# 512-column blocks for v, k, q and the output product, and the gate's modulation on TensorE

## The chip, the cores and the metric

One core of a Trainium2 chip runs one layer of a hybrid network as one program. The metric is the time of one execution on the device in microseconds (us), lower is better. Before the change three runs took 1288.12 to 1289.84 us, with a median of 1289.26 us.

## The reference, cut to what matters

All arithmetic is f32. There are 384 tokens (128 of a prompt with modulation vector `c_ctx`, 256 of a sample with `c`), `D_MODEL` is 2048, and the products below are the ones that the change touches.

```python
mod = jax.nn.silu(cond) @ w_ada + b_ada              # (2048) @ (2048, 6144)
shift, scale, gate = jnp.split(mod[:, None, :], 3, axis=-1)
proj = (_rms(x, norm_w) * (1 + scale) + shift) @ w_in
u, z_s, q, k, v, z_a, g_s, g_a = jnp.split(proj, cuts, axis=-1)   # q, k, v: 1024 columns each
q = _rms(q.reshape(n, L, N_HEADS, HEAD_DIM), q_norm_w)             # 16 heads of 64
k = _rms(k.reshape(n, L, N_HEADS, HEAD_DIM), k_norm_w)
...                                                    # state space branch, attention branch
merged = sigmoid(g_s) * p_s + sigmoid(g_a) * p_a
return x + gate * (merged @ w_o)                        # w_o: (2048, 2048)
```

## The kernel before

Every large product is cut into blocks of 256 output columns, and the list `blocks` gives the order in which TensorE goes through them: the rest of the gate columns (`gs`), v, `ga`, `za`, k and q in turn, then `glu`, `ps` (the state space output), `pa` (the attention output) and `wo` (the output product). A block reads its weights in units of 512 KB; a unit has two halves, and one half is one step of the main loop at the end of `hybrid`.

An f32 product is made from three fp32r products. `Stream.prep` (lines 59 to 66) splits each half of weights into a high part `hi` (a copy on ScalarE, line 64) and a low part `lo` (a subtraction, line 65), and the activations were split earlier into `hh` and `hl`. TensorE then adds high by high, high by low and low by high in PSUM. `mode_b` (lines 174 to 188) holds the weights still and moves 384 tokens past them. `mode_a` (lines 190 to 203) holds 128 tokens still and moves the weights; it serves v, k, q and wo. In `mode_a` a half is two slices of 128 rows by 256 columns, for three token tiles: 18 matmuls of 256 columns. The three token tiles share two PSUM banks of the pool `psm`, which has three; two tiles lie side by side in the first.

The low part is made on VectorE, except where `low_on_pool` is set: in the first stage and from `pa` on it is made on GpSimd.

Other work is written as generators and is put between the steps by `Background.step`: after each step every generator emits what is due, and `finish` drains one at once. The attention starts a head every two steps, once the k, q and v blocks that hold it are there. `split_ys` reads the state space result back and splits it for `glu`; it is started in the middle of the last q block, and `enter("glu")` calls `finish` on it. `keep` normalises one k or q block and turns it.

The gate's part of the modulation (2048 columns of `w_ada`, for both vectors) runs beside `pa` and `wo`. In `gate_step` (line 1269) a `w_ada` tile `gw` of 512 KB is loaded every second step, and each step does two VectorE operations `acc = gw * ct + acc` of 128x512, one for each vector; after 16 steps `gate_rows` splits `acc`, sums its 128 rows with a matmul against ones, and copies the result to `gt`. `evac` of a wo block multiplies the PSUM result by `gt`, adds x and stores it.

All loads and stores named here are issued by SyncE, in program order, in one line.

Of the kernel before, what the change touches and what calls it, by code (L numbers as in the profile page):

```python
# [6 lines left out]
F32 = mybir.dt.float32  # L7
# [27 lines left out]
class Stream:  # L35
# [11 lines left out]
    def load(self, i):  # L47
# [4 lines left out]
        elif kind == "k2":  # L52
            t = t.rearrange("p (k h) c -> p k (h c)", k=2)
            self.nc.sync.dma_start(t, dram(w, k0 * ncol + c0, [[ncol, 128], [128 * ncol, 2], [1, 512]]))
        else:
            self.nc.sync.dma_start(t.rearrange("p k c -> p (k c)"), dram(w, k0 * ncol + c0, [[ncol, 128], [1, 1024]]))
        self.loaded.append(t)

    def prep(self, j):
        i, b = divmod(j, 2)  # L60
        t = self.loaded[i][:, 2 * b:2 * b + 2, :] if self.units[i][4] != "k2" else self.loaded[i][:, :, 256 * b:256 * b + 256]
# [59 lines left out]
def hybrid(ctx, tc, a):  # L121
# [35 lines left out]
    mhalf = const.tile([128, 16], F32, name="mhalf")  # L157
# [32 lines left out]
    def mode_a(i, hb, ps, act, k0, first, last):  # L190

        wh, wl = st.split[2 * i + hb]
        xh, xl = act
        for r in range(3):
            tk = slice(128 * r, 128 * r + 128)
            o = ps[r // 2][:, 256 * (r % 2):256 * (r % 2) + 256]
            for kk in range(2):
                q, j = divmod(k0 + 2 * hb + kk, 4)
                z = last and hb == 1 and kk == 1
                PE.matmul(o, xh[q][:, j, tk], wh[:, kk, :], start=first and hb == 0 and kk == 0 and r != 1, stop=False,  # L200
                          skip_group_check=True)
                PE.matmul(o, xh[q][:, j, tk], wl[:, kk, :], start=False, stop=False, skip_group_check=True)  # L202
                PE.matmul(o, xl[q][:, j, tk], wh[:, kk, :], start=False, stop=z and r != 0, skip_group_check=True)  # L203
# [427 lines left out]

    for j in range(4, 8):
        block("gs", w_in, NIN, 6144 + 256 * j, 4)
    for j in range(4):
        block("v", w_in, NIN, 4096 + 256 * j, 4)
# [4 lines left out]
    for j in range(4):  # L640
        for kind, c0 in (("k", 3072), ("q", 2048)):
            block(kind, w_in, NIN, c0 + 256 * j, 4)
# [6 lines left out]
    for j in range(8):  # L649
        block("wo", a["w_o"], 2048, 256 * j, 4)  # L650
# [243 lines left out]
    def heads_norm(kvt, kr, c0, dst):  # L894

        def gen():
            sq = kvt.tile([128, 3, 256], F32, name="sq", bufs=1)
            r = kvt.tile([128, 12], F32, name="rn")
            r2 = kvt.tile([128, 12], F32, name="rm")
# [8 lines left out]
            tt(k3, k3, r2.unsqueeze(2).to_broadcast([128, 12, 64]), OP.mult)  # L908
            yield -1
            for j in range(2):  # L910
# [4 lines left out]
                dst(2 * c0 + j, p[:, :TOK].rearrange("p (r t) -> p r t", r=3))  # L915
# [4 lines left out]
    def attention(at, kS, kP, qT, vN, aT, ready, done):  # L920
# [118 lines left out]
        while len(start) < NH or tick - start[NH - 1] <= 15:  # L1039
            h = len(start)  # L1040
            if h < NH and (h == 0 or tick - start[h - 1] >= 2) and {("k", h // 4), ("q", h // 4), ("c", h // 4),
                                                                    h // 4} <= ready:
# [37 lines left out]
    def keep(kr, j, kind):  # L1080
        yield from heads_norm(kvt, kr, j, put_k if kind == "k" else put_q)
        M["vd"].add((kind, j))
        if kind == "k":
            kp = kr[:, 1].rearrange("p (h d) -> p h d", d=64)
            tt(kp, kp, kw.unsqueeze(1).to_broadcast([128, kp.shape[1], 64]), OP.mult)
            SP.dma_start(dram(a["out_k"], 256 * j, [[1024, 128], [1, 256]]), kr[:, 1])
# [11 lines left out]
    def evac(kind, c0, ps):  # L1098
        if kind in ("k", "q"):
            j = c0 % 1024 // 256  # L1100
# [3 lines left out]
            g_qk.append(bg.add(keep(kr, j, kind)))  # L1104
            return
        if kind == "v":
            j = c0 % 1024 // 256
            cs = slice(256 * j, 256 * j + 256)
            for r in range(3):
                S.activation(M["v"][r][:, cs], ps[r // 2][:, 256 * (r % 2):256 * (r % 2) + 256], AF.Copy)  # L1110
            SP.dma_start(dram(a["out_v"], 256 * j, [[1024, 128], [1, 256]]), M["v"][1][:, cs])
            M["vd"].add(j)
            return
        if kind == "wo":
            cs = slice(c0, c0 + 256)
            yt = M["gp"].tile([128, 3, 256], F32, name="yt", bufs=2)
            gt = M["gt"]
            for r, (n, t0) in enumerate((("out_s", 0), ("out_p", 0), ("out_s", 128))):
                tt(yt[:, r], ps[r // 2][:, 256 * (r % 2):256 * (r % 2) + 256], gt[:, r % 2, cs], OP.mult)
                tt(yt[:, r], yt[:, r], M["x"][:, r], OP.add)  # L1120
                SP.dma_start(dram(a[n], t0 * D + c0, [[D, 128], [1, 256]]), yt[:, r])
            return
        for c in range(2):
# [25 lines left out]
            elif kind == "pa":  # L1149
# [3 lines left out]
                tt(o, o, t, OP.add, eng=GP)  # L1153

    def enter(kind):
# [38 lines left out]
        elif kind == "pa":  # L1194
# [6 lines left out]
            one = gp.tile([128, 128], F32, name="one")  # L1201
            V.memset(one, 1.0)
            M["ones"] = gp.tile([128, 128], F32R, name="ones")
            S.activation(M["ones"], one, AF.Copy)
            M["bg"] = gp.tile([128, D], F32, name="bg")
            GP.memset(M["bg"], 0.0)
            SP.dma_start(M["bg"][0:1, :], dram(a["b_ada"], 4096, [[D, 1], [1, D]]))
# [61 lines left out]
    def gate_step(t):  # L1269

        gp = M["gp"]
        if t % 2 == 0 and t < 64:
            w = gaw[t // 2] = gp.tile([128, 2, 512], F32, name="gw", bufs=6)
            n, u = divmod(t // 2, 8)
            SP.dma_start(w, dram(a["w_ada"], 256 * u * 6144 + 4096 + 512 * n, [[6144, 128], [128 * 6144, 2], [1, 512]]))
        n, kt = divmod(t - 6, 16)
        if 0 <= n < 4:
            if kt == 0:
                gaw["acc"] = gp.tile([128, 2, 512], F32, name="acc", bufs=2)
            w = gaw[(t - 6) // 2][:, kt % 2]  # L1280
            for m in range(2):
                o = gaw["acc"][:, m]
                stt(o, w, ct[:, kt, m:m + 1], o if kt else M["bg"][:, 512 * n:512 * n + 512], OP.mult, OP.add)
            if kt == 15:
# [89 lines left out]
```

## Time and profile before

| what | value |
|---|---|
| median of 3 runs | 1289.26 us (1288.12 to 1289.84) |
| the profiled execution | 1288.84 us, of which 1287.1 us is the span from first to last instruction |
| TensorE busy | 1200.3 us (93%) |
| VectorE busy | 871.0 us (68%) |
| ScalarE, GpSimd busy | 574.7 us (45%), 326.2 us (25%) |
| mean granted TensorE clock | 0.981 of full speed |

The profile is of one execution. Busy times are sums over the whole span, and stages differ, so a share of the span says little about one stage. The granted clock of 1.00 is 2.4 GHz and 0.50 is 1.2 GHz; a value between them is a mean over a stretch that had both. Matmuls overlap each other, so what one costs is read from the distance between the starts of neighbours, not from its own duration.

### The profile page before, as it was taken

The numbers are of one execution on the slowest core, as the hardware profiler recorded it, in microseconds if no ns is written. First come the engines' busy times: TensorE is split into PE (matmuls) and PEld (weight loads), VectorE is DVE, ScalarE is ACT, GpSimd is POOL, SyncE is SP. The second block draws the span as 40 slices with busy tenths as digits, with TensorE's granted clock in tenths as the row PEclk, the third lists the DMA queues.
The fourth block names the chain that finished last, engine by engine and source line by source line (L and its number), as shares of the span: only waits on it lengthen the run. The fifth ranks groups of instructions, "written<-read, shape, count | busy, mean of one in ns | idle before, by whom it ended". The sixth has DMA issues, their size and how long they took to land.

```text
span 1287.1 us, 22729 instructions
## 1 busy us (share of the span) xinstructions
PE 1200.3 (93%) x8591; PEld 1109.6 (86%) x8591; DVE 871.0 (68%) x1931; ACT 574.7 (45%) x1060; POOL 326.2 (25%) x240
## 2 busy tenths in 40 slices
PE   3999999998999999999999999998999988778998
PEld 3787788897899988989997998987889987778898
DVE  3588765576479943649993446466786479999941
ACT  4432223335853378673349545455554233322231
POOL 2444445541000000000000001000100077766554
PEclk9999999999999999999999999999999999889999
DMA  9975566569264485337443555648673466656642
GB/s 266 349 268 196 199 217 232 162 147 262 68 158 157 140 146 150 95 90 174 151 153 106 155 121 123 103 111 198 172 180 130 156 205 216 221 163 230 228 145 92
DMA packets 256221, 219.97 MB, mean 171 GB/s; under 512 B 81319, under 2 KB 235551, under 8 KB 255727
## 3 DMA queue, kind: packets, MB, share of 16 engines
q1 hardware_dynamic: 255760, 218.33, 58.7%
q8 instruction: 68, 1.11, 0.4%
q0 software_dynamic: 352, 0.20, 0.2%
q14 instruction: 41, 0.34, 0.1%
HBM read 200.30 MB, written 16.87 MB: 169 GB/s over the span
## 4 chain that ended last, share of the span: by engine, by line
PE 68%; DVE 14%; DMA 6%; ACT 5%; issue 4%; SPq 2%; POOL 0%; DVEq 0%; ACTq 0%; POOLq 0%
PE m L186 8%; PE m L188 8%; PE m L187 8%; DVE acc L149 8%; PE m L200 7%; PE m L202 7%; PE m L203 6%; PE m L808 5%; PE m L809 5%; PE m L810 4%; PE bk L688 3%; PE bk L967 2%; DMA sg<-yss 2%; PE bk L443 1%; ACT H L454 1%
## 5 line engine op out<-in xcount | busy, mean ns | idle before, releaser
L64 ACT ACTIVATE hi<-raw 128x512 fp32r<-128x512 f32 x464 | 286.5, 628 | 381.9 <-PE m L203 122.0
L65 POOL TENSOR_TENSOR lo<-raw,hi 128x512 fp32r<-128x512 f32 x191 | 274.0, 1447 | 331.4 <-ACT hi L64 206.0
L65 DVE TENSOR_TENSOR lo<-raw,hi 128x512 fp32r<-128x512 f32 x273 | 186.6, 687 | 180.7 <-ACT hi L64 171.7
L186 PE MATMUL m<-hh,hi 128*128 128x384 f32 x832 | 289.5, 348 | 15.5 <-DVE tgl L149 12.9
L200 PE MATMUL m<-hi,hh 128*128 128x256 f32 x960 | 278.0, 290 | 16.2 <-DVE yt L141 14.3
L188 PE MATMUL m<-hh,lo 128*128 128x384 f32 x832 | 281.7, 339 | 1.0 <-POOL lo L65 0.9
L187 PE MATMUL m<-hl,hi 128*128 128x384 f32 x832 | 281.2, 338 | 0.0
L203 PE MATMUL m<-hi,hl 128*128 128x256 f32 x960 | 273.9, 285 | 1.0 <-DVE hl L149 1.0
L202 PE MATMUL m<-lo,hh 128*128 128x256 f32 x960 | 274.0, 285 | 0.1
L200 PEld LDWEIGHTS m<-hi,hh 128*128 128x128 f32 x960 | 186.3, 194 | 21.8 <-DVE yt L141 15.1
L203 PEld LDWEIGHTS m<-hi,hl 128*128 128x128 f32 x960 | 186.4, 194 | 1.2 <-DVE hl L149 1.2
L202 PEld LDWEIGHTS m<-lo,hh 128*128 128x128 f32 x960 | 186.5, 194 | 0.6 <-DVE lo L65 0.3
L186 PEld LDWEIGHTS m<-hh,hi 128*128 128x128 f32 x832 | 158.1, 190 | 27.6 <-DVE tgl L149 14.8
L188 PEld LDWEIGHTS m<-hh,lo 128*128 128x128 f32 x832 | 158.3, 190 | 2.2 <-POOL lo L65 1.8
L187 PEld LDWEIGHTS m<-hl,hi 128*128 128x128 f32 x832 | 158.5, 191 | 0.1
L808 PE MATMUL m<-hh,hi 128*128 128x384 f32 x384 | 135.1, 352 | 16.3 <-DVE hh L726 7.4
L149 DVE SCALAR_TENSOR_TENSOR acc<-gw,ct,acc 128x512 f32<-128x512 f32 x120 | 144.4, 1265 | 0.0
L809 PE MATMUL m<-hl,hi 128*128 128x384 f32 x384 | 131.2, 342 | 0.8 <-DVE hl L141 0.5
L810 PE MATMUL m<-hh,lo 128*128 128x384 f32 x384 | 130.7, 340 | 0.5 <-POOL lo L65 0.5
L141 POOL TENSOR_TENSOR rm<-rn,mhalf 128x12 f32<-128x12 f32 x8 | 19.1, 2386 | 380.8 <-PE m L203 229.9
L808 PEld LDWEIGHTS m<-hh,hi 128*128 128x128 f32 x384 | 73.1, 190 | 31.7 <-DVE hh L726 8.7
L809 PEld LDWEIGHTS m<-hl,hi 128*128 128x128 f32 x384 | 73.5, 191 | 2.2 <-DVE hl L141 2.2
(254 smaller groups left out, 1378.7 us busy)
## 6 DMA issues: line engine op xcount, KB each, us to landing
raw<-in_w_in_dram SPq DMA_DIRECT2D x160, 512.0 KB, 4.2
wa<-in_w_ada_dram SPq DMA_DIRECT2D x32, 1024.0 KB, 5.5
gw<-in_w_ada_dram SPq DMA_DIRECT2D x32, 512.0 KB, 6.5
raw<-in_w_o_dram SPq DMA_DIRECT2D x32, 512.0 KB, 6.2
raw<-in_w_ssm_out_dram SPq DMA_DIRECT2D x16, 512.0 KB, 3.5
raw<-in_w_att_out_dram SPq DMA_DIRECT2D x16, 512.0 KB, 5.6
br<-rpb SPq DMA_DIRECT2D x64, 64.0 KB, 7.4
raw<-in_w_glu_dram SPq DMA_DIRECT2D x8, 512.0 KB, 7.2
```

The costliest lines, as they stand in the source:

```text
L64: self.nc.scalar.activation(h, t, AF.Copy)
L65: (self.nc.gpsimd if self.low_on_pool else self.nc.vector).tensor_tensor(l, t, f(h), op=OP.subtract)
L149: return V.scalar_tensor_tensor(o, x, s, y, op0=op0, op1=op1)
L186: PE.matmul(o, wh[:, kk, w], xh[q][:, j, :], start=first and hb == 0 and kk == 0, stop=False)
L187: PE.matmul(o, wh[:, kk, w], xl[q][:, j, :], start=False, stop=False)
L188: PE.matmul(o, wl[:, kk, w], xh[q][:, j, :], start=False, stop=last and hb == 1 and kk == 1)
L200: PE.matmul(o, xh[q][:, j, tk], wh[:, kk, :], start=first and hb == 0 and kk == 0 and r != 1, stop=False, skip_group_check=True)
L202: PE.matmul(o, xh[q][:, j, tk], wl[:, kk, :], start=False, stop=False, skip_group_check=True)
L203: PE.matmul(o, xl[q][:, j, tk], wh[:, kk, :], start=False, stop=z and r != 0, skip_group_check=True)
L808: PE.matmul(o, wh[:, w], hh[q][:, j, :], start=kk == 0, stop=False)
L809: PE.matmul(o, wh[:, w], hl[q][:, j, :], start=False, stop=False)
L810: PE.matmul(o, wl[:, w], hh[q][:, j, :], start=False, stop=kk == nk - 1)
```

## The change

Three things change.

The products v, k, q and wo go over to blocks of 512 columns (`block_a`, weight kind "a"). A unit is then 256 rows by 512 columns, still 512 KB, and a half is one slice of 128 rows by 512 columns. Each token tile has a PSUM bank of its own, so such a block takes all three banks of `psm`. A half has 9 matmuls of 512 columns instead of 18 of 256. Evacuation, normalisation and stores go by 512 columns. `kr` has one buffer, and `evac` drains the previous `keep` before it writes it. The attention waits for groups of 8 heads where it waited for 4.

The gate's sum moves from VectorE to TensorE. Every fourth step four plain f32 matmuls, each with 32 columns of `ct` as weights and 512 columns of `gw` moving, write to four groups of 32 partitions of one bank; four such quads make 512 columns of gate. `gate_rows` then adds the bias, splits the sum once for both vectors, and a matmul against `sel` picks and adds the four rows of a vector.

The low parts in `pa` and `wo`, and the sum of the two branches in `pa`, move from GpSimd to VectorE.

```diff
-            o = ps[r // 2][:, 256 * (r % 2):256 * (r % 2) + 256]
-            for kk in range(2):
-                q, j = divmod(k0 + 2 * hb + kk, 4)
-                PE.matmul(o, xh[q][:, j, tk], wh[:, kk, :], start=..., stop=False, ...)
-                PE.matmul(o, xh[q][:, j, tk], wl[:, kk, :], start=False, stop=False, ...)
-                PE.matmul(o, xl[q][:, j, tk], wh[:, kk, :], start=False, stop=z and r != 0, ...)
+            PE.matmul(ps[r], xh[q][:, j, tk], wh, start=first and hb == 0, stop=False)
+            PE.matmul(ps[r], xh[q][:, j, tk], wl, start=False, stop=False)
+            PE.matmul(ps[r], xl[q][:, j, tk], wh, start=False, stop=last and hb == 1)
...
+    def block_a(kind, w, ncol, c0, nk):
+        blocks.append((kind, c0, nk, [st.add(w, ncol, 256 * q, c0, "a") for q in range(nk)]))
...
-            kr = kvt.tile([128, 3, 256], F32, name="kr")
-            S.activation(kr[:, 0:2].rearrange("p r c -> p (r c)"), ps[0], AF.Copy)
-            S.activation(kr[:, 2], ps[1][:, 0:256], AF.Copy)
+            if "keep" in M:
+                bg.finish([M["keep"]])
+            kr = kvt.tile([128, 3, 512], F32, name="kr", bufs=1)
+            for r in range(3):
+                S.activation(kr[:, r], ps[r], AF.Copy)
...
+            for r in range(3):
+                tt(yt[:, r], ps[r], gt[:, r % 2, cs], OP.mult)
             for r, (n, t0) in enumerate((("out_s", 0), ("out_p", 0), ("out_s", 128))):
-                tt(yt[:, r], ps[r // 2][:, 256 * (r % 2):256 * (r % 2) + 256], gt[:, r % 2, cs], OP.mult)
                 tt(yt[:, r], yt[:, r], M["x"][:, r], OP.add)
...
-                tt(o, o, t, OP.add, eng=GP)
+                tt(o, o, t, OP.add)
...
-        n, kt = divmod(t - 6, 16)
-        if 0 <= n < 4:
-            w = gaw[(t - 6) // 2][:, kt % 2]
-            for m in range(2):
-                o = gaw["acc"][:, m]
-                stt(o, w, ct[:, kt, m:m + 1], o if kt else M["bg"][...], OP.mult, OP.add)
+        quad, r = divmod(t - 8, 4)
+        if r == 0 and 0 <= quad < 16:
+            n, u = divmod(quad, 4)
+            if u == 0:
+                gaw["p"] = bank()
+            for g in range(4):
+                PE.matmul(gaw["p"][32 * g:32 * g + 32, :], ct[:, 4 * u + g, :], gaw[2 * quad + g // 2][:, g % 2],
+                          start=u == 0, stop=u == 3)
+            if u == 3:
+                bg.add(gate_rows(n, gaw["p"]), True)
...
-            if kind == "pa":
-                st.low_on_pool = True
-        ps = [psm.tile([128, 512], F32, name="m") for c in range(2)]
+        ps = [psm.tile([128, 512], F32, name="m") for c in range(3 if kind in ("k", "q", "v", "wo") else 2)]
...
-            if kind == "q" and c0 == 2816 and u == 2:
+            if kind == "q" and c0 == 2560 and u == 4:
                 enter("act")
-            if kind == "wo" and c0 == 0 and u == 2:
+            if kind == "wo" and c0 == 0 and u == 4:
                 bg.finish(g_mg)
```

How the order moves at three places. First VectorE in `pa`, before; `acc` is the gate's sum, `hl` a low part of the merged result, `tgl` a gate of the attention branch:

```order
L149 SCALAR_TENSOR_TENSOR acc<-gw,ct,acc 128x512 x2
L149 SCALAR_TENSOR_TENSOR hl_104<-ms_8242,hh_100 128x384
L149 SCALAR_TENSOR_TENSOR tgl<-tgl,m 128x384 x2
L149 SCALAR_TENSOR_TENSOR acc<-gw,ct,acc 128x512 x6
```

The same engine in `pa` now, where one `gate_rows` falls; `acc<-bk,bg` reads the gate's PSUM bank:

```order
L155 SCALAR_TENSOR_TENSOR tgl<-tgl,m 128x384
L147 TENSOR_TENSOR ms_7950<-ms_7950,tgl 128x384
L71 TENSOR_TENSOR lo<-raw,hi 128x512 x2
L147 TENSOR_TENSOR acc<-bk,bg 128x512
L71 TENSOR_TENSOR lo<-raw,hi 128x512 x2
L147 TENSOR_TENSOR gl<-acc,gh 128x512
L155 SCALAR_TENSOR_TENSOR tgl<-tgl,m 128x384
```

The two `acc` operations of each step are gone from VectorE, and the low parts `lo` and the sums `ms`, which GpSimd made, stand there.

Second TensorE in `pa` now, at a quad (nothing stood between the steps of `mode_b` there before):

```order
L192 MATMUL m<-hh_98,hi 128x384
L193 MATMUL m<-hl_102,hi 128x384
L194 MATMUL m<-hh_98,lo 128x384
L1291 MATMUL bk<-gw,ct 32x512 x4
```

The quad is in TensorE's own line, and what follows it waits until its `gw` tiles have landed.

Third ScalarE at the end of the last q block, before; `kr<-m` evacuates that block, `hh<-sg` belongs to `split_ys`, `sc` to the attention, and the first `hi` of the list belongs to `glu`:

```order
L1102 ACTIVATE kr<-m 128x512
L1103 ACTIVATE kr<-m 128x256
L1230 ACTIVATE hh_99<-sg 128x384 x2
L984 ACTIVATE sc_10433,mx<-sc_10433,mx 128x384
L986 ACTIVATE sc_10433,mx<-sc_10433,mx 128x128
L984 ACTIVATE sc_10451,mx<-sc_10451,mx 128x384
L901 ACTIVATE sq<-kr 128x768
L64 ACTIVATE hi<-raw 128x512
```

And now:

```order
L1240 ACTIVATE hh_99<-sg 128x384 x2
L1014 ACTIVATE PT<-bk 128x3x128
L989 ACTIVATE sc_9264,mx<-sc_9264,mx 128x384
L991 ACTIVATE sc_9264,mx<-sc_9264,mx 128x128
L70 ACTIVATE hi<-raw 128x512
...
L989 ACTIVATE sc_9387,mx<-sc_9387,mx 128x384
L1110 ACTIVATE kr<-m 128x512 x3
```

The last pair of `split_ys` stood behind the evacuation of the last q block and ahead of the attention's rows; it now stands four `hi` rows ahead of that evacuation.

## Rows read from the trace of the kernel before

**Rows 1.** The page, the chain that ended last, by engine.
```profile
PE 68%; DVE 14%; DMA 6%; ACT 5%; issue 4%; SPq 2%; POOL 0%; DVEq 0%; ACTq 0%; POOLq 0%
```
**Rows 2.** Stretches: length, then busy PE, PEld, DVE, ACT, POOL, clock, DMA share, GB/s.
```profile
387.30:456.40 69.10, 69.10 (x578) 69.10 (x577) 64.71 (x230) 23.50 (x44) 0.00 (x0) 1.00 0.45 142
721.30:890.70 169.40, 169.40 (x1313) 155.07 (x1312) 92.85 (x227) 83.32 (x191) 16.51 (x7) 1.00 0.60 130
890.70:910.40 19.70, 14.87 (x58) 11.85 (x57) 14.83 (x47) 10.31 (x28) 4.38 (x2) 0.74 0.87 291
1028.70:1117.30 88.60, 74.82 (x390) 71.82 (x389) 80.91 (x76) 27.41 (x49) 68.36 (x46) 0.94 0.65 212
1117.30:1287.10 169.80, 147.85 (x1166) 145.89 (x1164) 125.02 (x144) 46.24 (x78) 98.38 (x65) 0.95 0.54 175
```
**Rows 3.** TensorE in order of time: start, duration; matmuls of 512 and 256 columns.
```profile
1103.79 0.39 PE L1302 MATMUL bk<-gh,ones 128*128 128x512 f32 x1
...
1104.24 0.34 PE L186 MATMUL m<-hh,hi 128*128 128x384 f32 x1
...
1196.47 0.28 PE L200 MATMUL m<-hi,hh 128*128 128x256 f32 x1
...
1196.95 0.28 PE L202 MATMUL m<-lo,hh 128*128 128x256 f32 x1
```
**Rows 4.** Waits of TensorE from 1028 us on: total, times, longest.
```profile
PE m L200 <- DVE yt L141: 14.3, 4, 5.7
PE m L186 <- DVE tgl L149: 12.9, 6, 3.2
```
**Rows 5.** Groups: busy us, mean ns of one | idle before. The first from 1028.7 us on.
```profile
L149 DVE SCALAR_TENSOR_TENSOR acc<-gw,ct,acc 128x512 f32<-128x512 f32 x120 | 144.4, 1265 | 0.0
...
L65 DVE TENSOR_TENSOR lo<-raw,hi 128x512 fp32r<-128x512 f32 x273 | 186.6, 687 | 180.7 <-ACT hi L64 171.7
L141 DVE TENSOR_TENSOR yt<-m,gt 128x256 f32<-128x256 f32 x24 | 10.0, 416 | 40.9 <-PE m L203 40.9
L1304 ACT ACTIVATE gt<-bk 128x512 f32<-128x512 f32 x8 | 4.8, 600 | 17.5 <-PE bk L1302 17.5
```
**Rows 6.** TensorE in order of time around f32 matmuls, side by side and alone.
```profile
48.39 0.33 PE L810 MATMUL m<-hh,lo 128*128 128x384 f32 x1
...
48.91 0.34 PE L810 MATMUL m<-hh,lo 128*128 128x384 f32 x1
49.18 1.07 PE L688 MATMUL bk<-wa,ct 128*32 128x256 f32 x16
50.18 0.44 PE L808 MATMUL m<-hh,hi 128*128 128x384 f32 x1
50.46 0.34 PE L809 MATMUL m<-hl,hi 128*128 128x384 f32 x1
...
889.94 0.81 PE L967 MATMUL bk<-kS,qT 64*128 64x384 f32 x2
890.68 0.44 PE L186 MATMUL m<-hh,hi 128*128 128x384 f32 x1
```
**Rows 7.** TensorE and ScalarE in order of time where `glu` begins.
```profile
897.87 1.11 PE L999 MATMUL bk<-ident,sc 128*128 128x128 f32 x4 [4.83 <-DVE sc L145]
...
894.14 1.62 ACT L1230 ACTIVATE hh<-sg 128x384 fp32r<-128x384 f32 x2 [4.29 <-DMA sg<-yss]
```
**Rows 8.** The end of the program in order of time.
```profile
1282.05 0.28 PE L203 MATMUL m<-hi,hl 128*128 128x256 f32 x1
...
1284.16 0.33 SPq L1121 DMA_DIRECT2D out_s_dram<-yt  x1
```
**Rows 9.** The gate's loads: landing time, and the DMA line of SyncE around 1140 us.
```profile
gw<-in_w_ada_dram SPq DMA_DIRECT2D x32, 512.0 KB, 6.5
...
1133.12 0.37 SPq L51 DMA_DIRECT2D raw<-in_w_o_dram  x1
1146.47 0.36 SPq L1121 DMA_DIRECT2D out_s_dram<-yt  x1
```

More of the change, by code (lines that the diff above doesn't have):

```diff
@@ L156, in hybrid @@
         ts(ident, jp, 0.0, OP.is_equal)
-    mhalf = const.tile([128, 16], F32, name="mhalf")
+    mhalf = const.tile([128, 24], F32, name="mhalf")
     V.memset(mhalf, -0.5)
@@ L190, in mode_a @@
     def mode_a(i, hb, ps, act, k0, first, last):
[L192 removed]
+        wh, wl = (x.rearrange("p k c -> p (k c)") for x in st.split[2 * i + hb])
         xh, xl = act
+        q, j = divmod(k0 + hb, 4)
         for r in range(3):
             tk = slice(128 * r, 128 * r + 128)
[L196 to L203 removed]
+            PE.matmul(ps[r], xh[q][:, j, tk], wh, start=first and hb == 0, stop=False)
+            PE.matmul(ps[r], xh[q][:, j, tk], wl, start=False, stop=False)
+            PE.matmul(ps[r], xl[q][:, j, tk], wh, start=False, stop=last and hb == 1)
     def expo(pl, o, x, n):
@@ L639, in hybrid @@
         block("za", w_in, NIN, 5120 + 256 * j, 4)
-    for j in range(4):
+    for j in range(2):
         for kind, c0 in (("k", 3072), ("q", 2048)):
-            block(kind, w_in, NIN, c0 + 256 * j, 4)
+            block_a(kind, w_in, NIN, c0 + 512 * j, 8)
     for j in range(4):
@@ L648, in hybrid @@
         block("pa", a["w_att_out"], 2048, 256 * j, 2)
-    for j in range(8):
-        block("wo", a["w_o"], 2048, 256 * j, 4)
+    for j in range(4):
+        block_a("wo", a["w_o"], 2048, 512 * j, 8)
     M = {"aT": set(), "vd": set()}
@@ L1200, in enter @@
             M["gt"] = gp.tile([128, 2, D], F32, name="gt")
[L1201 to L1204, printed above, removed]
+            pick = gp.tile([128, 2], F32, name="pick")
+            V.tensor_reduce(pick, ident.rearrange("p (g x) -> p x g", x=32)[:, 0:2], axis=AX.X, op=OP.add)
+            M["sel"] = gp.tile([128, 2, 128], F32R, name="sel")
+            V.tensor_copy(M["sel"], pick.unsqueeze(2).to_broadcast([128, 2, 128]))
             M["bg"] = gp.tile([128, D], F32, name="bg")
             GP.memset(M["bg"], 0.0)
-            SP.dma_start(M["bg"][0:1, :], dram(a["b_ada"], 4096, [[D, 1], [1, D]]))
+            SP.dma_start(M["bg"][0:2, :], dram(a["b_ada"], 4096, [[0, 2], [1, D]]))
             M["tg"] = []
@@ L1300, in gate_rows @@
             p = bank()
-            for i in range(2):
-                PE.matmul(p, M["ones"], parts[m][i], start=i == 0, stop=i == 1)
+            for i, part in enumerate((h, l)):
+                PE.matmul(p, M["sel"][:, m], part, start=i == 0, stop=i == 1)
             yield -1
```

85 lines of the change are left out of this document (43 added, 42 removed).

## The prediction, made before the changed kernel was run

> **What bounds the kernel now.** I read the chain that ended last first [rows 1]: TensorE holds 68% of it, VectorE 14%. Then I cut the span into stages [rows 2]. In the v stage and the k/q stage TensorE is busy for the whole stretch at full clock, so only fewer or shorter matmuls help there. The last two stretches, `pa` and `wo`, differ: VectorE is busy for 80.9 of 88.6 us and 125.0 of 169.8 us, TensorE has idle time, and its granted clock is 0.94 and 0.95, which means that it fell to 1.2 GHz now and then. The waits of TensorE there [rows 4] all lead to VectorE: 14.3 us for the evacuation `yt` in wo, 12.9 us for `tgl` in pa. The reason stands in the groups [rows 5]: 120 `acc` operations of 1.265 us, 144.4 us on VectorE in a line in which the evacuations queue behind them. So three stretches are bound by TensorE's work (v, k/q, most of the rest) and the last 254 us by VectorE's line.
>
> To count what TensorE needs, I take the distance between starts [rows 3]: 0.120 us for 256 columns (four from 1196.47 to 1196.95) and 0.225 for 512 (two from 1103.79 to 1104.24). For 384 it is 0.1735 (three in 0.52 us from 48.39 to 48.91 [rows 6]). The straight line through 256 and 384 gives 0.227 at 512; I take that.
>
> **The change part by part.**
>
> *Wider matmuls.* v had 576 matmuls of 256 columns and now has 288 of 512: 576 x 0.120 = 69.1 us becomes 288 x 0.227 = 65.4, a gain of 3.7 us. k and q together have twice that, 7.4 us, and wo again 7.4 us. The first two lie on TensorE's path fully, since it has no idle time there; the third counts once wo is bound by TensorE. The bounds: nothing, if 512 costs twice 256, and 0.002 us more each if 0.225 holds. The Trainium skill, "TensorE: Matmul & The Clock Gate", section "Back-to-back issue gap", gives N/2.4 plus 2.5 ns for a warm matmul: 109 ns at 256 and 216 at 512. By it a pair would save 2.6 ns, all 1440 pairs 3.7 us instead of 18.5. The trace does not agree at 256: it has 120 ns.
>
> *The gate's sum.* 128 VectorE operations leave. What TensorE loses by them is read from the sum: from 1028.7 to the end of the last matmul at 1282.2 [rows 8] are 253.5 us, and its work is 384 x 0.1735 = 66.6 in pa, 1152 x 0.120 = 138.2 in wo and 16 x 0.227 = 3.6 for `gate_rows`, 208.4 us. So 45.1 us are lost, 27.2 in the waits of [rows 4] and the rest in smaller waits and in matmuls at half clock after them. This is the largest term, and all of it can go: VectorE had 205.9 us of work in the two stretches; it loses 144.4, gains 96 `lo` of 0.687 [rows 5] = 66.0 and 16 narrower branch sums, under 11 us, and so has at most 139 us in about 225. Nothing of that is long enough to hold an evacuation back by itself. I leave 5 us of waits for places I can't see (0 to 12).
>
> *The quads on TensorE.* They are new and on the path. The nearest row is the same form in the first stage [rows 6]: eight f32 matmuls of 256 columns with 32 columns of weights (16 records) take 1.00 us, with 0.27 instead of 0.17 before them and 0.28 instead of 0.17 after: 1.20 us in all. Four of 512 columns move as many columns, so a quad costs 1.2 us, and 16 quads 19.2 us. Below: 1.00 each, 16 us. Above: if the four did not run side by side. The nearest f32 matmul that stands alone has 384 columns and takes 0.74 us to the start of the next (889.94 to 890.68 [rows 6]); at 512 that is 0.99, and four in a line 3.9 us. The eight of the row, half as wide, would have taken 3.9 us too; they took 1.00, so they do run side by side, and 1.2 is what I take.
>
> *Three banks per block.* A block now takes every bank of `psm`, where before one bank was free for the next. The first matmul of a block waits for the evacuation of token tile 0. The last half of a block goes tile by tile, three matmuls each, so tile 0 is complete 6 x 0.227 = 1.36 us before the block ends. Its evacuation costs 0.60 us on ScalarE (the 512-column row of `gt`) and, doubling 0.416, 0.83 us on VectorE at most [rows 5]; tile 1 then has to be free 0.68 us after the new block starts and tile 2 at 1.36. Each is ready in time, or within 0.1 us of it, if the engine comes to it at once. I take zero, and bound it by all three evacuations, 1.8 to 2.5 us, at each of the 10 block ends.
>
> *`glu`.* TensorE waits 4.8 us where `glu` begins [rows 7], since the attention's `sc` stands on ScalarE behind a `split_ys` row that waits 4.3 us for its DMA; the stretch has a clock of 0.74 [rows 2], so about 10 us ran at half speed, which cost some 3.5 more (at most half of what TensorE worked in it). In the new order that row stands four `hi` rows earlier with a whole step of TensorE work between each, so the DMA wait is covered by about 14 us of matmuls and attention. I take 6 us of the 8.3 (0 to 8.3).
>
> *Costed at nothing.* The attention of a group of 8 heads starts later; its last product stands 108 matmuls (18.7 us) ahead of `pa`, which covers it, and its TensorE work is the same wherever it is put. `finish` on `keep` finds it done, with seven steps (14 us) to spare. The memset of `bg` waits for attention tiles, with the same 18.7 us. *The end.* The last evacuation does three products before the first sum; with rows twice as wide the last store is issued later, about 1 us.
>
> **The sum**, against the profiled execution's 1288.84 us: -3.7 (v) -7.4 (k, q) -7.4 (wo) -45.1 (lost time in pa and wo) +19.2 (quads) +5 (left waits) -6 (`glu`) +1 (end) = -44.4, so 1244.4 us. The median of the runs shown is 0.4 us higher; I forecast 1245.
>
> **The rivals.**
>
> *The wait moves to the banks.* If the evacuating engine is late, each of the 10 ends of blocks costs about 2 us: 1245 + 20 = 1265. For it: in the attention's steps ScalarE has a dense line, and the k/q evacuation stands behind `sc` rows. Against: there the attention's own matmuls follow the block and give time.
>
> *A wide matmul costs two narrow ones.* Then the 18.5 us of the first part stay away: 1263. Against: 0.225 for the two in [rows 3], where double would be 0.240. The skill's formula above comes near this: 14.8 us less gain, 1260. By that rule 384 columns would take 162 ns, and the trace has 173.5.
>
> *The quads run one after the other.* Then a quad takes 3.9 us, and 16 cost 43 us more: 1288, no change. Against: [rows 6].
>
> *Slower than before: TensorE waits for `gw`.* It is TensorE that now needs the gate's weights, in its own line, in 16 places. A `gw` lands 6.5 us after issue [rows 9] and is issued six steps, at least 12.5 us, ahead. But SyncE issues in one line, and there is a hole of 13.3 us in it before, in which a store waited for `yt` and the loads behind it stood [rows 9]. If each quad comes to wait, the gain of 44 us is used up at 2.8 us per quad. Waits cost clock too: 0.94 and 0.95 over the last two stretches [rows 2] mean 28 us at half speed for some ten waits, so it could decide from 1.4 us on. At 4 us each: 1309. Against: the store waited for the VectorE line that goes away; and the rate, 212 GB/s in pa at a DMA share of 0.65, need rise to only about 265 GB/s in the shorter stage, while another stretch shows 291 [rows 2].
>
> *The change gives more:* no left waits, all of `glu`, cheaper quads: 1245 - 5 - 2 - 3 = 1235.
>
> **How the numbers follow.** Forecast, 1236 to 1256: 0.74. Banks: 0.09. Wide matmuls at double cost: 0.05. Quads one by one: 0.02 (no change). `gw` late: 0.05. More than forecast: 0.05. The range 1233 to 1265 reaches over the case of more gain and both cases around 1264; beyond it lie the last two rivals and the tails. A measurement of this kernel tells 0.2%, some 2.6 us, from no change. The other cases are faster: 0.93, same 0.02, slower 0.05.
>
> **What would show it.** In the v stretch 288 matmuls 0.227 us apart and about 65 us in all. In pa and wo TensorE close to gap-free, a granted clock of 1.00, waits for `yt` and `tgl` under 5 us in total, VectorE busy for about 60% and GpSimd nearly empty. Quads 1.2 us from the matmul ahead to normal pace, with no DMA named as releaser. At the start of `glu` no wait of several us. I am wrong if TensorE's waits name an evacuation at every block end, if a quad's row carries idle time released by `gw`, or if the starts of 512-column matmuls are 0.24 apart.

## The result and the profile after

The changed kernel takes 1257.9 us (median of four runs, 1256.5 to 1260.0); the kernel before took 1288.7 beside it. The ratio is 0.976, with a 95% interval from 0.9745 to 0.9781. The forecast was 1245: of the 44 us that the sum promised 31 came.

The profiled execution has a span of 1255.4 us, 31.7 less than before. First the chain that ended last, by engine, which answers to [rows 1]:

```profile
PE 77%; ACT 8%; DVE 6%; DMA 4%; issue 3%; POOL 1%; SPq 0%; DVEq 0%; ACTq 0%; POOLq 0%
```

VectorE's share fell from 14% to 6%, and TensorE's rose from 68% to 77%: what the change aimed at has happened. Now the stretches, with the columns of [rows 2]. The first is the v stage, the second runs from the first matmul of k to the first of pa, the third is pa, the last runs from wo to the end.

```profile
386.90:452.28 65.38, 65.38 (x290) 54.04 (x289) 63.00 (x228) 23.18 (x38) 0.00 (x0) 1.00 0.48 148
708.28:1028.06 319.78, 309.77 (x1547) 252.22 (x1546) 192.15 (x459) 150.47 (x343) 19.84 (x5) 0.98 0.58 144
1028.06:1102.88 74.82, 74.82 (x437) 68.11 (x437) 42.33 (x75) 26.38 (x46) 0.00 (x0) 1.00 0.82 265
1102.88:1255.40 152.52, 145.87 (x669) 110.97 (x668) 65.86 (x103) 45.42 (x75) 0.00 (x0) 0.99 0.56 187
```

The second of these stretches in the kernel before:

```profile
712.31:1028.73 316.42, 311.18 (x2122) 282.71 (x2121) 194.16 (x473) 151.34 (x350) 20.90 (x9) 0.98 0.60 146
```

Set the forecast beside these lengths:

| stretch | before | after | forecast | measured |
|---|---|---|---|---|
| up to v | 387.3 | 386.9 | 0 | -0.4 |
| v to k (v, ga, za) | 325.0 | 321.4 | -3.7 | -3.6 |
| k to pa (k, q, glu, ps) | 316.4 | 319.8 | -13.4 | +3.4 |
| pa to the end of the span | 258.4 | 227.3 | -27.3 | -31.0 |
| span | 1287.1 | 1255.4 | -44.4 | -31.7 |

Three lines agree within 4 us. The miss lies in one, k to pa: by the prediction's count TensorE has 7.4 us less work there, and the stretch takes 3.4 us more. That line is what the experiments are about. TensorE in order of time: the start of v, two places of that stretch, and a quad in pa:

```profile
388.98 0.39 PE L203 MATMUL m<-hi,hh 128*128 128x512 f32 x1
389.21 0.39 PE L204 MATMUL m<-lo,hh 128*128 128x512 f32 x1
...
893.44 0.87 PE L918 MATMUL bk<-ident,kr 128*128 128x128 f32 x3 [2.73 <-DVE kr L147]
...
934.56 0.34 PE L194 MATMUL m<-hh,lo 128*128 128x384 f32 x1
939.36 0.69 PE L192 MATMUL m<-hh,hi 128*128 128x384 f32 x1 [4.46 <-DVE ms L155]
939.84 0.52 PE L193 MATMUL m<-hl,hi 128*128 128x384 f32 x1
940.16 0.52 PE L194 MATMUL m<-hh,lo 128*128 128x384 f32 x1
...
1046.87 1.06 PE L1291 MATMUL bk<-gw,ct 128*32 128x512 f32 x8
1047.87 0.45 PE L192 MATMUL m<-hh,hi 128*128 128x384 f32 x1
```

The 512-column matmuls start 0.23 us apart, and a quad takes 1.00 us plus its edges, as forecast. The new thing is the wait of 4.46 us in ps. TensorE names VectorE's `ms`, the evacuation of a ps block; that one stood in a queue, so the next step is VectorE's own line, and behind it ScalarE and the DMA line of SyncE:

```profile
928.31 0.69 DVE L71 TENSOR_TENSOR lo<-raw,hi 128x512 fp32r<-128x512 f32 x1
934.26 0.56 DVE L147 TENSOR_TENSOR sg<-sg,qT 128x384 f32<-128x384 f32 x1 [5.27 <-DMA sg<-zas]
...
934.85 0.52 ACT L1097 ACTIVATE hh<-sg 128x384 fp32r<-128x384 f32 x1 [5.33 <-DVE sg L147]
...
915.31 4.08 SPq L961 DMA_DIRECT2D br<-rpb  x4
919.43 0.60 SPq L51 DMA_DIRECT2D raw<-in_w_ssm_out_dram  x1
920.08 4.65 SPq L961 DMA_DIRECT2D br<-rpb  x4
924.83 1.12 SPq L51 DMA_DIRECT2D raw<-in_w_ssm_out_dram  x1
926.05 0.45 SPq L1252 DMA_DIRECT2D sg<-zas  x1
926.55 5.04 SPq L961 DMA_DIRECT2D br<-rpb  x4
```

The first `zas` load, with which `gate_att` gates the attention's output, was issued at 926.05 and used at 934.26. VectorE stood behind it for 5.27 us, and with it `lo` of the next weights, the evacuation `ms` and the softmax. Ahead of the load and directly behind it in SyncE's line stand `br` loads, four for a head, which bring the attention's position bias. Landing times of both kinds between 860 and 1010 us (median us in the last column):

```profile
br<-rpb SPq DMA_DIRECT2D x32, 64.0 KB, 7.4
...
sg<-zas SPq DMA_DIRECT2D x8, 192.0 KB, 8.2
```

In the kernel before, the median of the eight `zas` loads was 5.0 us, and they came after the last `br`: the attention was further along when ps began. But the first of them, the one that counts here, was no faster then:

```profile
944.81 4.83 SPq L956 DMA_DIRECT2D br<-rpb  x4
...
950.94 3.02 SPq L1242 DMA_DIRECT2D sg<-zas  x1
...
960.72 0.56 DVE L141 TENSOR_TENSOR sg<-sg,qT 128x384 f32<-128x384 f32 x1 [0.20 <-DMA sg<-zas]
```

It landed some 9.8 us after its issue, and VectorE came to it after 9.6, so it waited 0.20 us. Now the first load lands after 8.2 us, and VectorE comes to it after 2.9 (926.05 to 929.0). By the program both kernels use it two steps after asking for it, and in both the pair of heads that it gates was long done (six of the eight pairs were done before, four are now). What has shrunk is the time between its issue and its use.

After both waits TensorE runs at half clock for a while. The stretches behind them:

```profile
893.44:896.67 3.23, 3.23 (x12) 3.23 (x12) 1.75 (x3) 1.10 (x2) 0.00 (x0) 0.50 0.55 158
939.36:947.80 8.44, 8.44 (x25) 7.18 (x26) 6.98 (x23) 2.37 (x6) 0.00 (x0) 0.50 0.83 181
```

A granted clock of 0.50 is 1.2 GHz. At that level the 384-column matmuls start 0.32 us apart (939.84 to 940.16), at 2.4 GHz 0.1735. If half of these two stretches is counted as lost, an estimate is that the wait of 4.46 us cost some 8.7 us in all, and that of 2.73 us some 4.3.

### The profile page after: what moved, and what is told of

It is laid out like the page before. It is cut to its first block, busy times and chain, and to the rows that moved or that the text cites. A ratio compares the mean times of both kernels' runs of the same rounds, so it can differ in the third digit from the quotient of the medians.

```text
span 1255.4 us, 19839 instructions
## 1 busy us (share of the span) xinstructions
PE 1192.1 (95%) x7279; PEld 1025.7 (82%) x7279; DVE 770.3 (61%) x1876; ACT 572.2 (46%) x1041; POOL 158.6 (13%) x126
## 3 DMA queue, kind: packets, MB, share of 16 engines
q1 hardware_dynamic: 231250, 218.33, 59.6%
## 4 chain that ended last, share of the span: by engine, by line
PE 77%; ACT 8%; DVE 6%; DMA 4%; issue 3%; POOL 1%; SPq 0%; DVEq 0%; ACTq 0%; POOLq 0%
PE m L192 10%; PE m L194 10%; PE m L193 10%; PE m L203 8%; PE m L205 7%; PE m L204 7%; PE m L813 5%; PE m L814 5%; PE m L815 5%; PE bk L693 2%; DMA sg<-yss 2%; ACT H L456 2%; PE bk L972 1%; PE bk L1291 1%; ACT hi L70 1%
## 5 line engine op out<-in xcount | busy, mean ns | idle before, releaser
L71 DVE TENSOR_TENSOR lo<-raw,hi 128x512 fp32r<-128x512 f32 x367 | 249.8, 687 | 261.7 <-ACT hi L70 257.4
L203 PE MATMUL m<-hi,hh 128*128 128x512 f32 x480 | 190.8, 398 | 0.0
L204 PE MATMUL m<-lo,hh 128*128 128x512 f32 x480 | 187.2, 390 | 0.1
L205 PE MATMUL m<-hi,hl 128*128 128x512 f32 x480 | 187.3, 390 | 0.0
L194 PEld LDWEIGHTS m<-hh,lo 128*128 128x128 f32 x832 | 157.5, 189 | 0.9 <-DVE lo L71 0.9
L71 POOL TENSOR_TENSOR lo<-raw,hi 128x512 fp32r<-128x512 f32 x97 | 126.6, 1313 | 152.0 <-ACT hi L70 146.1
L203 PEld LDWEIGHTS m<-hi,hh 128*128 128x128 f32 x480 | 90.1, 188 | 28.0 <-ACT hi L70 5.0
L205 PEld LDWEIGHTS m<-hi,hl 128*128 128x128 f32 x480 | 90.1, 188 | 19.3
L204 PEld LDWEIGHTS m<-lo,hh 128*128 128x128 f32 x480 | 90.2, 188 | 18.2 <-DVE lo L71 0.5
L815 PEld LDWEIGHTS m<-hh,lo 128*128 128x128 f32 x384 | 73.6, 192 | 0.9 <-POOL lo L71 0.9
L147 POOL TENSOR_TENSOR rm<-rn,mhalf 128x24 f32<-128x24 f32 x4 | 18.0, 4508 | 368.7 <-DVE rn L152 368.7
```

Of the source, the lines that this page charges most:

```text
L71: (self.nc.gpsimd if self.low_on_pool else self.nc.vector).tensor_tensor(l, t, f(h), op=OP.subtract)
L194: PE.matmul(o, wl[:, kk, w], xh[q][:, j, :], start=False, stop=last and hb == 1 and kk == 1)
L203: PE.matmul(ps[r], xh[q][:, j, tk], wh, start=first and hb == 0, stop=False)
L204: PE.matmul(ps[r], xh[q][:, j, tk], wl, start=False, stop=False)
L205: PE.matmul(ps[r], xl[q][:, j, tk], wh, start=False, stop=last and hb == 1)
L815: PE.matmul(o, wl[:, w], hh[q][:, j, :], start=False, stop=kk == nk - 1)
```

## The experiments

The theory to be tested (A): what the wide blocks won ahead of pa was lost again, because a group of eight heads is ready later and the second half of the attention came to lie beside glu and ps. Rivals: the wide blocks cost by themselves (B), the waits are crowding and no single load is to blame (C), the later attention costs nothing (D). Whole times are compared with their medians. Stretches are taken from the profiles: the time at which k begins differs by 4.5 us between profiles of kernels that are the same up to there (707.2 to 711.7), so spans alone would mislead. A stretch is of one profile each, so a difference of one or two us between stretches is not told from noise.

### The change in halves

The gate's part alone, on the kernel before:

```diff
-                tt(o, o, t, OP.add, eng=GP)
+                tt(o, o, t, OP.add)
-            if kind == "pa":
-                st.low_on_pool = True
 (gate_step, gate_rows, sel and bg as in the change; every block of 256 columns)
```

> The kernel before with the gate's part of the change alone: modulation in quads on TensorE, lo and the last add of pa on VectorE; v, k, q and the output product stay in blocks of 256 columns. Theory A (what the wide blocks won ahead of pa was lost again, because the attention's second half moved into the ps stage beside the step that gates the attention's output): the pa and wo stages lose their 45.1 us of gaps and pay 16 quads of 1.23 us, 1288.7 - 45.1 + 19.7 = 1263 us (1260 to 1266); the pa stage begins where it did before, at 1028 to 1029 us. Rival B (the wide blocks gain nothing anywhere and the gate alone made the whole difference): 1258 us.

Measured: 1263.3 us, ratio 0.9795 (0.9778 to 0.9812). Its stretches k to pa, pa, and wo to the end:

```profile
714.07:1029.42 315.35, 310.62 (x2122) 282.33 (x2121) 194.07 (x473) 152.08 (x351) 20.89 (x9) 0.99 0.59 146
1029.42:1104.26 74.84, 74.84 (x437) 68.15 (x437) 42.36 (x75) 26.39 (x46) 0.00 (x0) 1.00 0.83 272
1104.26:1261.90 157.64, 152.92 (x1245) 142.49 (x1244) 68.63 (x127) 45.41 (x75) 0.00 (x0) 1.00 0.55 179
```

That is theory A's number; rival B had 1258. (pa begins at 1029.4, a little behind the 1028 to 1029 expected.) Of the 31 us the gate alone brings 26. Against the changed kernel, wo to the end is 5.1 us longer (157.6 against 152.5), which is the gain of wide products in wo, less the later last store.

The wide blocks alone, with the gate as before (and five buffers for its weights, for want of room):

```diff
 (gate_step, gate_rows, ones and bg as before the change)
+            if kind == "pa":
+                st.low_on_pool = True
-                tt(o, o, t, OP.add)
+                tt(o, o, t, OP.add, eng=GP)
```

> The changed kernel with the gate back as it was: modulation summed on VectorE, lo and the last add of pa on GpSimd; the wide blocks stay. Five buffers for the modulation's weights in place of six, for want of room beside the wider tiles. Theory A: v ends 4 us earlier, k and q save 12 us, the stages glu and ps give 15 us of it back, so pa begins within 1 us of 1028.7; in pa and wo VectorE sets the pace as before and the wider products win little: 1285 us (1281 to 1289). Rival B (the wide blocks cost by themselves, by banks or by the longer evacuation): above 1290 us.

Measured: 1287.8 us, ratio 0.9994 (0.9982 to 1.0007): by themselves the wide blocks bring nothing that can be measured. pa begins at 1027.1, 1.6 us sooner than before where 1 was expected, and in the last two stretches TensorE waits for VectorE as in [rows 4], and in wo now for GpSimd's `lo` too:

```profile
PE m L192 <- DVE tgl L155: 13.9, 6, 3.3
PE m L203 <- DVE yt L147: 10.2, 2, 5.2
PE m L204 <- POOL lo L71: 5.7, 4, 3.4
```

A holds. The wide products of wo pay only once VectorE and GpSimd no longer set the pace there. One thing more differs in this run, the five buffers in place of six; no run shows what they do alone.

### Undoing k and q alone

```diff
-    for j in range(2):
+    for j in range(4):
         for kind, c0 in (("k", 3072), ("q", 2048)):
-            block_a(kind, w_in, NIN, c0 + 512 * j, 8)
+            block(kind, w_in, NIN, c0 + 256 * j, 4)
 (heads_norm, the evacuation and the groups of four heads as before; v, wo and the gate as changed)
```

> The changed kernel with k and q alone back in blocks of 256 columns, the heads again in groups of 4 with the normalisation in tiles of 256 columns; v, wo and the gate as changed. Theory A (the attention's later start costs 19.4 us between k/q and pa and takes away the 8.4 us stall at the start of glu): 1257.9 + 7.4 for the narrow products - 19.4 + 8.4 = 1254 us (1251 to 1257). Rival D (the later attention costs nothing, and the time lies elsewhere): 1257.9 + 7.4 = 1265 us, or up to 1274 with the stall at glu back.

Measured: 1254.7 us (0.9716 to 0.9746 of before), 3.2 us less than the changed kernel: taking that part of the change back makes it faster. k to pa is 315.0 us, about as before the change (316.4). D, by which it would have been 1265 us or more, falls.

### The late load

`gate_att` asks for its loads four ahead in place of two:

```diff
-        for k in range(10):
+        for k in range(12):
             if k < 8:
                 zt[k] = stg.tile([128, TOK], F32, name="sg")
                 SP.dma_start(zt[k], zas[k])
-            if k >= 2:
+            if k >= 4:
 (k - 4 for k - 2 below)
```

> The changed kernel with the loads of the attention's stored gates (zas) issued four ahead of their use in the ps stage in place of two; nothing else. Theory A (VectorE stood 5.3 us behind the first of these loads at 929 us, and with it the low halves of the weights and TensorE): the stall at 933 to 950 us goes, 8.7 us of it, 1250 us (1248 to 1253). Rival C (the stall is crowding, the attention's own work at that place, and the load only the last to be seen): the wait moves to another releaser and the time stays, 1257 us (1255 to 1259).

Measured: 1248.7 us, ratio 0.9682 (0.9665 to 0.9698), 9.2 us less than the changed kernel. k to pa takes 311.2 us instead of 319.8. The place of the stall:

```profile
931.20:943.00 11.80, 11.80 (x60) 9.66 (x60) 9.59 (x32) 4.70 (x13) 0.00 (x0) 1.00 0.81 162
```

TensorE is busy throughout at full clock. C falls for this stall: one load, asked for too late, held three engines. The loads themselves are no faster (8.7 us in the median); they are only not waited for.

What the `br` loads have to do with it is the question of a kernel that leaves out half of them for the last eight heads:

```diff
-            for qt in range(2):
+            for qt in range(2 if h < 8 else 1):
                 for r2 in range(2):
                     SP.dma_start(br[h][64 * r2:64 * r2 + 64, qt], ...)
-                tt(bw, br[h][:, qt, :, ::-1], ...)
+                tt(bw, br[h][:, qt if h < 8 else 0, :, ::-1], ...)
```

> The changed kernel with half of the position bias loads (br, two of four for a head) of heads 8 to 15 left out, the other half used in both places. It asks why the zas loads land 8.2 us after their issue, where it was 5.0 before and is 3.8 with narrow k and q. Theory A1 (they lie behind and beside the br loads of the second eight heads): landing falls to 5 or 6 us, the stall at 933 to 950 us shrinks by half or more, 1251 to 1254 us. Rival (the weight stream delays them, or they are simply asked for too late): landing stays above 7.5 us, 1257 us.

Measured: 1251.2 us (two runs, 1250.5 to 1252.0); k to pa 311.0 us, the stall is gone whole. SyncE's line and VectorE's at that place, and the landing of the first `zas` load here and in the changed kernel:

```profile
916.71 1.24 SPq L961 DMA_DIRECT2D br<-rpb  x2
...
918.64 2.79 SPq L961 DMA_DIRECT2D br<-rpb  x2
...
923.35 0.34 SPq L1252 DMA_DIRECT2D sg<-zas  x1
923.75 2.53 SPq L961 DMA_DIRECT2D br<-rpb  x2
...
927.02 2.37 SPq L1252 DMA_DIRECT2D sg<-zas  x2
...
930.29 0.68 DVE L71 TENSOR_TENSOR lo<-raw,hi 128x512 fp32r<-128x512 f32 x1
930.89 0.55 DVE L147 TENSOR_TENSOR sg<-sg,qT 128x384 f32<-128x384 f32 x1
...
sg<-zas SPq DMA_DIRECT2D x1, 192.0 KB, 6.4
sg<-zas SPq DMA_DIRECT2D x1, 192.0 KB, 8.2
```

The first `zas` is the one issued at 923.35; it landed 6.4 us later and was used at 930.89 without a wait. This profile runs 2.0 us behind that of the changed kernel here (the `lo` ahead of the use starts at 930.29, there at 928.31). With that taken off, the load was issued 4.7 us sooner than in the changed kernel and landed 1.8 us faster, together more than the 5.27 us that VectorE had waited. So the larger part is SyncE's line: the two groups of `br` ahead of the load held it for 4.08 and 4.65 us, and with half the loads for 1.24 and 2.79, again 4.7 us less. The smaller part is a faster landing. A1 had both ("behind and beside"), though its landing of 5 to 6 us was missed: 6.4 for the first load, 7.0 in the median of the eight. Since half the `br` loads are gone on both sides of the load, this run doesn't tell which of them slowed its landing.

The `br` loads are read in rows of 64 numbers, 256 bytes. The Trainium skill, "DMA: Bandwidth & Descriptors", section "Why small descriptors are slow (HBM only)", puts the overhead of a 256-byte descriptor at 27%. No run here shows how much of the time in SyncE's line or of the landing is due to that.

### The normalisation's wait

The other new wait is for `kr`: the power on GpSimd takes 4.51 us for 24 columns (2.39 for 12 before), and the multiply of 1536 columns 1.75 us on VectorE. First two steps more for all four normalisations, on the kernel with the early loads:

```diff
             rsqrt_(r2, r)
-            yield -2
+            yield -4
```

> The kernel with the zas loads four ahead (1248.7 us), and the heads' normalisation two steps later behind its power on GpSimd (4.5 us for a tile of 512 columns, 2.3 us for one of 256): its multiply on VectorE and the transposes that follow wait two steps more. Theory A (TensorE waits 3.5 us for that multiply, and the two steps at 889 and 894 us take 5.2 and 5.8 us where their work takes some 3): 1244.5 us (1243 to 1246.5). Rival C (the work only moves, and another wait takes its place): 1248.5 us (1247 to 1250).

Measured: 1250.5 us (1247.1 to 1252.6): no gain. A's number, 1244.5, failed. The wait for `kr` is gone, and in its place the transposes meet the first eight heads' attention and wait for a bank:

```profile
852.57 0.90 PE L918 MATMUL bk<-ident,kr 128*128 128x128 f32 x3 [2.92 <-ACT PT L1014]
```

So the last normalisation alone was moved:

```diff
-            yield -2
+            yield -4 if last else -2
 (last: kind == "q" and j == 1)
```

> The kernel with the zas loads four ahead (1248.7 us), and two steps more between power and multiply in the normalisation of the last q block alone, the one whose transposes TensorE waits for (3.5 us); the three normalisations before it stay where they were, since moving all four sent the transposes into the first eight heads' attention, where they waited 2.9 us for a bank. Theory A (that wait is idle time and nothing else is due there): 1244.5 us (1243 to 1246.5). Rival C (the attention's second half, which starts two steps later, brings the time back): 1247 to 1250 us.

Measured: 1248.6 us (1244.4 to 1250.0), the same again. The two halves of k to pa, cut at the same step of glu (the eleventh of its sixteen), first this kernel, then the one with early loads only:

```profile
710.60:904.74 194.14, 191.97 (x919) 150.50 (x918) 112.62 (x249) 97.80 (x212) 18.03 (x4) 1.00 0.59 154
904.74:1020.89 116.15, 113.42 (x630) 96.88 (x629) 79.49 (x211) 52.33 (x132) 1.81 (x1) 1.00 0.61 139
```
```profile
708.95:907.20 198.25, 193.54 (x922) 152.31 (x920) 112.41 (x249) 98.59 (x214) 19.84 (x5) 0.99 0.57 151
907.20:1020.15 112.95, 112.15 (x626) 96.83 (x625) 79.68 (x212) 51.98 (x130) 0.00 (x0) 1.00 0.63 143
```

The first half gains 4.1 us, as A said, and the second loses 3.2: with the heads two steps later the waits that the trace lists there grow from 0.6 to 2.6 us, and 1.3 us of TensorE's work have moved into it. For this wait C was right.

### Do wide k and q pay at all?

Narrow k and q again, with the `yss` loads at glu's start asked for four ahead and two steps earlier, the way `zas` was mended for the wide ones:

```diff
-        for k in range(10):
+        for k in range(12):
 (split_ys uses k - 4 for k - 2, and waits four steps after the fourth load)
-            if kind == "q" and c0 == 2816 and u == 2:
+            if kind == "q" and c0 == 2816 and u == 0:
                 enter("act")
```

> The kernel with k and q in blocks of 256 columns (1254.7 us), and the loads of the recurrent layer's output (yss) that TensorE waits for at the start of glu issued four ahead of their use and two steps earlier. It asks whether wide blocks of k and q pay at all once the waits on either side are mended. Theory A (the stall at glu is 6.7 us of waiting for one load, as the profile of the narrow kernel shows): 1248 us (1247 to 1250), so that the wide k and q are worth the 3 to 4 us that are left of their 7.4. Rival D (the stall was covered by VectorE's work and stays under another name): 1254 us.

Measured: 1249.7 us (five runs, 1247.7 to 1254.7), by whole times not to be told from the wide kernel with its load mended, 1248.7. By k to pa the narrow one is 2.5 us shorter, 308.7 against 311.2, though its products cost 7.4 us more; this is one profile of each, and the narrow one's was the fastest of its five runs. So some 6 to 10 us stand against the wide blocks even with the late load mended. The parts of k to pa, in us:

| kernel | k and q | glu | ps |
|---|---|---|---|
| before | 178.4 | 59.6 | 78.4 |
| changed | 166.3 | 46.2 | 107.3 |
| changed, `zas` four ahead | 166.2 | 46.3 | 98.7 |
| narrow k and q, `yss` early | 177.8 | 50.5 | 80.4 |

The ps stage of the last two:

```profile
921.45:1020.15 98.70, 98.70 (x554) 84.34 (x553) 69.76 (x195) 44.76 (x116) 0.00 (x0) 1.00 0.61 140
938.08:1018.52 80.44, 79.67 (x459) 73.82 (x459) 51.53 (x120) 34.29 (x76) 0.00 (x0) 1.00 0.49 149
```

What the wide blocks win in the first two stages they give back in ps, where the attention's second half now lies: 554 matmul records against 459, TensorE busy for all of 98.70 us and at full clock, so no long wait is left there to mend. Over the whole of k to pa TensorE is idle for 5.5 us in the wide kernel and for 0.9 in the narrow one; 3.5 of that is the wait for `kr`, which is still in. And its busy time is only 2 us less (305.7 against 307.8), where the count of products says 7.4; some 1.6 us of that is the half clock after the wait for `kr`, and for the rest the traces name nothing. Whether the wide blocks bring the loss themselves (rival F of the next two runs) or only beside the attention (theory E) is asked of the same pair with the attention's work left out:

```diff
-        stages = sorted([(0, fetch), (5, masked), (14, mix), (15, mixed)] + ...)
+        stages = [(15, mark)]
 (mark only adds the pair of heads to done)
```

> The kernel with the zas loads four ahead and wide k and q, with all work of the attention left out (bias, scores, softmax, transposes, mixing); the projections, the heads' normalisation, the gating and everything after stay. Between the start of k and the start of pa there are then 576 products of 0.227 us, 576 of 0.1735 us and 56 transposes, 131 + 100 + 5 = 236 us. With the attention this stretch took 311.2 us, and 308.6 us with narrow k and q and their wait at glu mended, though narrow products cost 7.4 us more. Theory E (the 7.4 us are lost in crowding with the attention, which the wide order puts beside glu and ps): 237 to 241 us here, 6 to 8 us less than its narrow twin. Rival F (the wide blocks lose it by themselves, in evacuation and normalisation): 243 us or more, within 2 us of its twin.

> The twin with narrow k and q: the kernel with k and q in blocks of 256 columns and the yss loads early, all work of the attention left out as in the other. Its stretch from k to pa: 1152 products of 0.120 us, 576 of 0.1735 us, 56 transposes, 138 + 100 + 5 = 243 us. Theory E: 244 to 248 us, 6 to 8 us more than the wide one. Rival F: within 2 us of the wide one.

Measured: 1186.5 and 1193.4 us (two runs each). k to pa, first wide, then narrow:

```profile
711.65:959.34 247.69, 241.80 (x1211) 213.97 (x1210) 131.16 (x203) 110.36 (x198) 19.86 (x5) 0.99 0.54 169
```
```profile
707.15:963.17 256.02, 248.11 (x1787) 245.45 (x1785) 132.89 (x217) 111.43 (x206) 20.32 (x9) 0.99 0.52 164
```

The difference is 8.3 us, and 6.3 in TensorE's busy time. Both levels lie 7 to 8 us over the expected ones, in part for waits that I had not counted (4.3 us for `kr` in the wide one, 7.5 for `hi` in the narrow one). These waits differ too, so the cleaner number is that of the k and q stage alone, where neither has a long wait and both run at full clock:

```profile
711.65:850.35 138.70, 137.48 (x623) 111.82 (x622) 65.29 (x97) 65.59 (x119) 13.57 (x3) 1.00 0.50 154
707.15:851.23 144.08, 143.99 (x1204) 143.78 (x1203) 68.59 (x111) 68.71 (x129) 15.91 (x7) 1.00 0.45 140
```

That is 5.4 us, against the 7.4 counted and the 2 at most that F allowed: without the attention the wide blocks keep the larger part of their gain, and F falls as the whole cause. It is right in one thing: the wait for `kr` is there without the attention too, so the wide tile brings it by itself.

### The price of a quad

```diff
-            for g in range(4):
+            for g in range(4 if u == 3 else 0):
                 PE.matmul(gaw["p"][32 * g:32 * g + 32, :], ct[:, 4 * u + g, :], gaw[2 * quad + g // 2][:, g % 2],
-                          start=u == 0, stop=u == 3)
+                          start=True, stop=True)
```

> The changed kernel with 12 of the 16 quads of the gate's modulation left out (only the last four input tiles of each block of 512 columns are summed); the weights are loaded as before, the rest is unchanged. If a quad costs what the steps show (1.23 us each, nothing hidden): 1257.9 - 14.8 = 1243 us (1242 to 1245). Rival: part of a quad's time lies in gaps that stay without it, or the clock falls with the engine's less steady stream: 1246 to 1252 us.

Measured: 1240.9 us (1239.8 to 1244.4). From pa to the end of the span:

```profile
1029.90:1242.60 212.70, 206.04 (x1009) 177.87 (x1008) 108.31 (x177) 71.69 (x121) 0.00 (x0) 0.99 0.69 228
```

That is 14.6 us less than the 227.3 of the changed kernel, 1.22 us for each of the 12 quads that are left out: nothing of a quad is hidden. By the medians it is 17.0 us, 1.4 a quad, and just past the 1242 to 1245 expected; the profile is of the slowest of the four runs. What the 2.4 us between the two counts are, no trace here shows.

## Why the prediction came out as it did

The 1257.9 us lie past the 1236 to 1256 that had a chance of 0.74, and inside the wider range of 1233 to 1265. That range went so far up to cover two rivals, late banks and wide matmuls at double cost, and neither came: that the time lies in it is luck.

**Right, with their sizes.** v: -3.6 for -3.7. The quads: 1.22 us each for 1.2. The lost time in pa and wo: gone whole; TensorE is busy for 74.8 of 74.8 us in pa, its clock is 1.00 and 0.99, VectorE is busy for 43 to 57% of these stretches (about 60 was said) and GpSimd not at all. The wait at the start of glu: mending it in the narrow kernel took 6.3 us out of k to pa (315.0 to 308.7), and 5.0 by the medians (1254.7 to 1249.7), for 6; the changed kernel shows no wait at that place. None of the rivals came: the first matmuls of a block show no wait for an evacuation, and no quad waited for `gw`, which landed in 6.3 us.

**Mis-sized, small.** The 5 us of left waits in pa and wo: none are listed there. The end: from the start of the last matmul to the end of the span 7.0 us (1248.36 to 1255.4) instead of 5.0 (1282.05 to 1287.1), so 2.0 for 1. Together with the quads these make -31.0 of the -27.3.

**The step that failed** is "Costed at nothing". It said that the attention of a group of eight heads starts later and that its TensorE work is the same wherever it is put. The work is the same; what it stands beside is not. Of the 16.8 us between -13.4 and +3.4, 8.6 are the `zas` load (319.8 to 311.2 with loads four ahead), which is the wait of 4.46 us and the half clock after it. The prediction asked whether the attention would end in time for pa, and never what `gate_att` would meet at the start of ps: the `br` loads of the late heads stood ahead of its first load in SyncE's line, so VectorE came to that load 2.9 us after its issue, where it had been 9.6.

The other 8.2 us are about as much as the whole gain of k and q (7.4). Without the attention 5.4 of it is there, and with it nothing is left that whole times can tell (1248.7 against 1249.7). The one long wait in it is that for `kr`, 3.5 us, which comes with the normalisation of twice as many columns; the prediction counted nothing for that. Moving it away brought nothing back (1248.6 against 1248.7). That the rest goes in short waits where the attention, glu's evacuations and the splitting of weights share ScalarE and VectorE is not shown; where it goes stays open.

A version that beats both came out of it: the changed kernel with the `zas` loads four ahead, 1248.7 us.

## What to carry to other kernels

Work that is put later has the same cost on its own engine and can cost something else on the others: for each moved block, ask which loads and evacuations it will now stand beside, and how long before its use each of them is asked for. A distance of a fixed number of steps says little by itself: here the same two steps were 9.6 us before and 2.9 us after, for the larger part because other loads stood ahead in the same line, and the stall went through VectorE to ScalarE and TensorE. When a load is late, look at its own issue and landing, and not at the median of its kind: the median rose from 5.0 to 8.2 us while the first load, the one waited for, landed sooner than before. And a saving on TensorE is counted only after asking whether the engines that feed it have the same time left, as the wide blocks alone showed: -18.5 us of matmul work, nothing in the whole time.

## What the runs showed of the hardware

- Four 64 KB loads of 256-byte rows held SyncE's line for 4.08 to 5.04 us around 915 to 932 us of the changed kernel, and for 2.56 us at 905.65 us; pairs of them, in the kernel with half as many, for 1.24 to 2.79 us. With half as many, the load behind them was issued 4.7 us sooner.
- That load, of 192 KB, landed in 8.2 us, and in 6.4 us with half as many of them around it.
- A wait of 2.73 us on TensorE was followed by 3.2 us of work at 1.2 GHz (granted clock 0.50 from 893.44 to 896.67), one of 4.46 us by 8.4 us of it (0.50 from 939.36 to 947.80). With half of that counted as lost, the longer wait cost 8.7 us (an estimate), and mending it gave 8.6.
- The spacing at 1.2 GHz is 0.32 us for 384 columns. The formula for the cold clock in the Trainium skill, "TensorE: Matmul & The Clock Gate", section "Back-to-back issue gap", N/1.2, gives the same 320 ns, while its warm one gives 162 where the trace has 173.5.
- GpSimd's power takes about twice the time for twice the columns: 2.39 us for 12 and 4.51 for 24. It stands between two VectorE operations on which TensorE waits.
